# Rotary q and k turned by block squares and transfers instead of on TensorE, in a one-core decoder layer

## Chip, cores and metric

One NeuronCore of a Trainium2 chip runs the whole program. The metric is the device time of one execution in microseconds (us), as the median over runs. The core has five engines that run side by side, each with its own instruction queue: TensorE (PE, with its weight loads shown apart as PEld), VectorE (DVE), ScalarE (ACT), GpSimd (POOL) and SyncE (SP, which here only starts transfers).

## The reference

One layer of a decoder, on 256 tokens of width 1024, all in float32. A rotary mixer (branch a) and a stick-breaking mixer (branch b), both with 8 heads of 64, stand between two gated feed-forward halves:

```python
h = h + FFN_RES * swiglu(rms_norm(h, ffn1_norm), ffn1_w_gate, ffn1_w_up, ffn1_w_down)
u = rms_norm(h, mix_norm)
q_a, k_a, v_a, q_b, k_b, v_b, g_a, g_b = split(u @ w_in)
y_a = merge_heads(moba_attention(rotary(q_a), rotary(k_a), v_a))     # causal softmax
y_b = merge_heads(stick_breaking_attention(q_b, k_b, v_b))
gates = sigmoid(concatenate([g_a, g_b]) + b_gate)
h = h + (gate_a * (y_a @ w_branch_moba) + gate_b * (y_b @ w_branch_sb)) @ w_out
h = h + FFN_RES * swiglu(rms_norm(h, ffn2_norm), ffn2_w_gate, ffn2_w_up, ffn2_w_down)
out = rms_norm(h, final_norm)
```

The rotary turns the first 16 of each head's 64 columns by an angle that depends on the position.

## The kernel before

All weights are one stream of 376 tiles of 128x512. SP loads them in chunks of two tiles (512 KB) into `raw` buffers (`Weights.load`, L139 to L150; three buffers from chunk 12 on). `Weights.split` (L152) cuts each tile into a high part `wh` on ACT (L160 or L163) and the rest `wl` on DVE (L161 or L164), ten buffers of each. `unit` (L296) is the smallest step: three matmuls of 128x512, `wh` and `wl` by the activations' high part and `wh` by their low part (L292 to L294). After each unit `weave.tick()` counts one step and `W.pump()` splits one more tile, up to `AHEAD` = 7 tiles ahead of the tile in use. For 256 tokens each tile serves two units, t = 0 and t = 1.

The order of work on PE and SP is the order of the program, throughout. On ACT, DVE and POOL a planner sets the order in the middle of the kernel (from the end of the first feed-forward half to the start of the second) and the program in the rest. Side work is a set of Python generators in `Weave` (L92): each yields the number of steps after which it goes on, so `D_READY = 7` is a wait of seven units. Tasks added with `long=True`, the two attention lanes, advance at most one step between them per tick, and `flush(long=True)` runs whatever is left of them without units between.

Steps are counted here from the first unit of the mixer's input projection: blocks `in0` to `in9` of 16 units each (q_a, k_a, v_a, q_b, k_b, v_b and four blocks of gates, L874 to L890), so they are steps 1 to 160. Then come `ba` (y_a by its branch weights, steps 161 to 176, L901 to L917), `bb` (y_b, from step 177, L935 to L943) and `wo` (L948). In `in0` the t = 1 units come eight behind those of t = 0, elsewhere two; each block's two PSUM results (`acc_bank`, three buffers) are taken away by `evac`.

To be used in attention, q and k must stand with the head's columns on partitions. The kernel has two ways to turn them:

- For branch a (`rotary` true), `evac` copies the block to SBUF on ACT, `rotate` (L660) applies the rotary by four GpSimd operations (L666 to L669), and `turn` (L692) lets PE transpose eight 128x128 blocks by an identity into PSUM (L701), `D_TURN` = 10 steps after the second evacuation. ACT and DVE split the result into two parts (`split`, L312), and `D_READY` = 7 steps later it may be used.
- For branch b, DVE transposes 32x32 squares within 128x512 (L689) and `exchange` (L413) moves the squares between partitions by 16 transfers, alternately on SP's and GpSimd's queue, two a step. `D_LANDED` = 6 steps later the pieces are split.

The first column halves of the normalised activations after each feed-forward half and after the mixer go through `exchange` too (`Normed.moved`, L357: `uq`, `zq`); it puts 16 transfers of 16 KB a row block on the two queues.

The lanes (`lane`, L850) take head pairs 0 and 2, and 1 and 3: `moba_pair` (L765) for each as soon as q_a and k_a are there, then `stick_pair` (L809) as soon as q_b and k_b are. One `stick_pair` is scores `z`, three ACT operations, `sp`, cumulative sums (L834 to L836), the exponential `w` (L838), its split and `values` (L753), which makes `y_b`. The gates' sigmoids (L915) need another ACT table than the exponentials and are kept behind the last of them (`issue_after(marks["exp"])`).

`big` (L209) gives 24 SBUF buffers of 4 KB a partition to all the tiles of 128x1024.

Of the kernel before, what the change touches and what calls it, by code (L numbers as in the profile page):

```python
# [8 lines left out]
F32 = mybir.dt.float32  # L9
# [8 lines left out]
P = 128  # L18
# [10 lines left out]
CH = 2  # L29
# [8 lines left out]
D_TURNED = 3  # L38
D_MOVE = 2
D_MOVED = 12  # L40
D_LANDED = 6
D_PIECE = 2
D_TURN = 10
D_READY = 7
D_NORM = 4
D_SQUARES = 3
D_EIGHT = 6
# [81 lines left out]
class Weights:  # L129
# [9 lines left out]
    def load(self, n, tiles=0):  # L139

        n = min(n, N_TILES // CH)
        while self.loaded < n * CH + tiles:
            c, j = divmod(self.loaded, CH)
            if j == 0:
                nm = f"raw{c}"
                self.raw[c] = self.early(nm) if c < 12 else self.pool.tile([P, CH * 512], F32, name=nm, tag="raw", bufs=3)
            step = 1 if c < 4 else CH
            s = slice(j * 512, (j + step) * 512)
            self.nc.sync.dma_start(self.raw[c][:, s], self.stream[c, :, s])
            self.loaded += step  # L150

    def split(self):  # L152
        i = self.ready
        self.load(i // CH + 1)
        raw = self.raw[i // CH][:, i % CH * 512:i % CH * 512 + 512]
        hi = self.pool.tile([P, 512], F32R, name=f"wh{i}", tag="wh", bufs=self.bufs)
        lo = self.pool.tile([P, 512], F32R, name=f"wl{i}", tag="wl", bufs=self.bufs)
        g = self.gain(i)
        if g is None:
            self.nc.scalar.copy(hi, raw)  # L160
            self.nc.vector.tensor_sub(lo, raw, hi.bitcast(F32))  # L161
        else:
            self.nc.scalar.activation(hi, raw, AF.Copy, scale=g)  # L163
            self.nc.vector.scalar_tensor_tensor(lo, raw, g, hi.bitcast(F32), op0=ALU.mult, op1=ALU.subtract)  # L164
        self.parts[i] = hi, lo
        self.ready += 1
        if i % CH == CH - 1:
            del self.raw[i // CH]
            self.load(i // CH + 1 + 3)

    def pump(self):
        if self.ready < min(self.freed + self.bufs, self.at + self.ahead, N_TILES):
# [16 lines left out]
def hybrid_layer_kernel(ctx, tc, x, xt, pos, g_final, bgate, wstream, out):  # L189
# [17 lines left out]
        return psum.tile([P, 1024], F32, name=nm, tag="pr", bufs=2)  # L207

    def big(nm, dt=F32R):  # L209
        return work.tile([P, 1024], dt, name=nm, tag="big", bufs=24)  # L210

    def wide(nm, w=768):
        return work.tile([P, w], F32, name=nm, tag="f", bufs=4)
# [127 lines left out]
    class Normed:  # L341
# [15 lines left out]
        def moved(self, c):  # L357

            s = slice(c * 512, c * 512 + 512)
            q = big(f"{self.nm}q{self.t}{c}", F32)  # L360
            nc.vector.transpose(slots(q[:, 0:512], 4), plain(h[self.t][:, s]))
            yield D_SQUARES
            yield from exchange(q[:, 512:1024], q[:, 0:512], 4, [nc.sync, nc.gpsimd], 1)
            yield D_EIGHT
            split(plain(self.parts[0][:, s]), plain(self.parts[1][:, s]), slots(q[:, 512:1024], 4))
            self.there.add(c)
# [8 lines left out]
    class Given(Normed):  # L375
# [15 lines left out]
        def blk(self, k):  # L391
            o = k % 4 * T + self.t * P
            return [q[:, o:o + P] for q in self.made[k // 4 * 2:k // 4 * 2 + 2]]

    def lagged(n, lag):

# [9 lines left out]
    def slots(q, n):  # L406

        return q[:, 0:n * P].rearrange("p (g s w) -> p s g w", g=4, s=n)
# [15 lines left out]
    def ffn(base, xn, nm, on_half, lag, last=False):  # L424
# [5 lines left out]
        def hidden(b, t, bank):  # L430
# [10 lines left out]
            nc.vector.transpose(dst, plain(sh[:, 256:512]))  # L441
            if t == 1 and (b % 2 or b == FB - 1):
                weave.add(turn_hidden(p, n), D_TURNED)

        def later(f, *args):
            f(*args)
            return
            yield

        def turn_hidden(p, n):  # L450
            moved = big(f"hm_{nm}{p}", F32)
# [219 lines left out]
    def heads(b0, nm, res, rotary, diagonal):  # L671


        for j, which in enumerate("qk"):
            src = {}
            squares = None if rotary else big(f"{which}s{nm}", F32)

            def evac(t, ps, j=j, which=which, src=src, squares=squares):
                dst = row512(f"{which}{nm}{t}")
                if j == 0:  # L680
                    if nm == "a":
                        nc.gpsimd.tensor_scalar(rq[t], un[t].r, 0.125, None, op0=ALU.mult)
                    nc.scalar.activation(dst, ps, AF.Copy, scale=rq[t])
                else:
                    nc.scalar.activation(dst, ps, AF.Copy, scale=un[t].r)
                if rotary:
                    rotate(dst, t)
                else:
                    nc.vector.transpose(slots(squares, 8)[:, t:t + 7:2], plain(dst))  # L689
                src[t] = dst  # L690

            def turn(which=which, src=src, squares=squares):  # L692
                if rotary:
                    tp = two_banks(f"{which}tp{nm}")
                else:
                    tp = big(f"{which}m{nm}", F32)
                    yield from exchange(tp, squares, 8, [nc.sync, nc.gpsimd], 1)
                    yield D_LANDED
                for pr in range(4 if rotary else 0):
                    for t in range(2):  # L700
                        nc.tensor.transpose(tp[:, pr * 256 + t * P:pr * 256 + (t + 1) * P], src[t][:, pr * P:(pr + 1) * P], ident)  # L701
                if which != diagonal:
                    parts = big(f"{which}Th{nm}"), big(f"{which}Tl{nm}")
                    for c in range(2):
                        s = slice(c * 512, c * 512 + 512)
                        if rotary:
                            split(parts[0][:, s], parts[1][:, s], tp[:, s])
                        else:
                            split(plain(parts[0][:, s]), plain(parts[1][:, s]), slots(tp, 8)[:, c * 4:c * 4 + 4])
                            yield D_PIECE  # L710
                    ready = [[q[:, pr * 256:(pr + 1) * 256] for q in parts] for pr in range(4)]
                else:
                    tp4 = slots(tp, 8).rearrange("p (c t) g w -> p c t g w", t=2)
                    for c in range(2):
                        for j in range(2):
                            rows = slice(j * HD, j * HD + HD)
                            dst = [q[rows].rearrange("p (c j t g w) -> p c j t g w", c=2, j=2, t=2, g=4)[:, :, j] for q in res["bd"][c]]
                            split(dst[0], dst[1], tp4[rows, c * 2:c * 2 + 2])
                            yield D_PIECE
                    ready = [[q[:, pr % 2 * 512:pr % 2 * 512 + 512] for q in res["bd"][pr // 2]] for pr in range(4)]  # L720
                yield D_READY if rotary else D_READY - D_PIECE
                res[which] = ready

            if which == diagonal:
                res["bd"] = [(big(f"bdh{nm}{c}"), big(f"bdl{nm}{c}")) for c in range(2)]
                for c in range(2):
                    for q in res["bd"][c]:
                        for half in range(2):
                            q5 = q[half * HD:(half + 1) * HD].rearrange("p (c j t) -> p c j t", c=2, j=2)
                            nc.gpsimd.memset(q5[:, :, 1 - half, :].bitcast(F32), 0.0)  # L730
            project(b0 + j, evac)
            weave.add(turn(), D_TURN if rotary else D_TURNED)

        vs = big(f"vh{nm}"), big(f"vl{nm}")

        def evac_v(t, ps):
            s = slice(t * 512, t * 512 + 512)
            nc.scalar.activation(vs[0][:, s], ps, AF.Copy, scale=un[t].r)
            nc.vector.scalar_tensor_tensor(vs[1][:, s], ps, un[t].r, vs[0][:, s].bitcast(F32),
                                           op0=ALU.mult, op1=ALU.subtract)  # L740
            if t == 1:
                res["v"] = [[q[:, s * 512:(s + 1) * 512] for q in vs] for s in range(2)]

        project(b0 + 2, evac_v)
# [64 lines left out]
    def stick_pair(pr, b, y):  # L809
# [26 lines left out]
            nc.tensor.matmul(z0[:, :, 128:256], ones, s1, start=False, stop=i == 1, skip_group_check=True)  # L836
        w = wide(f"w{pr}")
        marks["exp"] = nc.scalar.activation(w, zz, AF.Exp).ins  # L838
        earlier(w)
        yield D_STICK[2]  # L840
        wh, wl = wide_r(f"wwh{pr}"), wide_r(f"wwl{pr}")
# [59 lines left out]
    for c in range(2):  # L901
        banks = {}
        for t, k in lagged(4, 2):
            if k == 0:
                banks[t] = acc_bank(f"ba{t}{c}")
            i = W_BR + c * 4 + k
            unit(banks[t], yk(ys["a"], k, t), W.get(i), k == 0, k == 3)
            if t == 1:
                W.done(i)
        if c == 0:  # L910
            weave.flush(long=True)
            with tc.issue_after(marks["exp"]):
                for br in range(2):
                    for t in range(2):
                        nc.scalar.activation(gates[br, t], gates[br, t], AF.Sigmoid)  # L915
        for t in range(2):
            nc.vector.tensor_mul(merged[t, c], banks[t], gate_half(0, t, c))  # L917

    mn = [None, None]

# [134 lines left out]
```

## Time and profile before

| | |
|---|---|
| median of 3 runs | 556.39 us (556.18 to 556.6) |
| the profiled execution's own time | 555.9 us |
| its span in the trace | 554.2 us |
| granted TensorE clock, mean over the span | 0.997 of full speed |
| busy share of the span: PE, PEld, DVE, ACT, POOL | 99%, 81%, 72%, 61%, 13% |
| DMA over the span | 111.69 MB, mean 202 GB/s |

The trace gives a start and a duration for each instruction. An engine that could not start has an idle time before it, and the trace names what ended it. Matmuls overlap in PE's pipeline, so a matmul's duration (390 ns for 512 columns) is more than its share of PE's time; the distance between the starts of two neighbours is that share. A row of a timeline with xN holds N instructions in a row. All numbers of an argument come from one profiled execution.

### The profile page before, as it was taken

The numbers are of one execution on the slowest core, as the hardware profiler recorded it, in microseconds if no ns is written. First come the engines' busy times: TensorE is split into PE (matmuls) and PEld (weight loads), VectorE is DVE, ScalarE is ACT, GpSimd is POOL, SyncE is SP. The second block draws the span as 40 slices with busy tenths as digits, with TensorE's granted clock in tenths as the row PEclk, the third lists the DMA queues.
The fourth block names the chain that finished last, engine by engine and source line by source line (L and its number), as shares of the span: only waits on it lengthen the run. The fifth ranks groups of instructions, "written<-read, shape, count | busy, mean of one in ns | idle before, by whom it ended". The sixth has DMA issues, their size and how long they took to land.

```text
span 554.2 us, 7853 instructions
## 1 busy us (share of the span) xinstructions
PE 546.1 (99%) x2494; PEld 449.5 (81%) x2494; DVE 401.3 (72%) x694; ACT 338.1 (61%) x576; POOL 70.1 (13%) x141
## 2 busy tenths in 40 slices
PE   9999999999999999999999999999999999999995
PEld 5788888888888888888888888888888888888884
DVE  6887788766466676889888888777677678655645
ACT  6865656655454767677875774476556566544633
POOL 1200000000003746022022200460000000000000
PEclk9999999999999999999999999999999999999998
DMA  8946766775685677455545464576657766757722
GB/s 311 403 141 202 220 216 216 220 237 184 210 235 179 200 232 220 155 159 183 176 151 172 137 202 149 179 242 216 219 180 234 238 206 200 229 179 230 243 79 76
DMA packets 42937, 111.69 MB, mean 202 GB/s; under 512 B 8080, under 2 KB 16528, under 8 KB 42896
## 3 DMA queue, kind: packets, MB, share of 16 engines
q1 hardware_dynamic: 40464, 107.90, 60.9%
q0 software_dynamic: 2000, 2.62, 1.8%
q10 hardware_dynamic: 432, 0.67, 0.3%
q8 instruction: 19, 0.31, 0.3%
q14 instruction: 22, 0.18, 0.1%
HBM read 102.25 MB, written 1.05 MB: 186 GB/s over the span
## 4 chain that ended last, share of the span: by engine, by line
PE 95%; DMA 3%; ACT 0%; DVE 0%; issue 0%; ACTq 0%
PE gu_f L293 14%; PE gu_f L294 14%; PE gu_f L292 14%; PE dn_f L294 7%; PE dn_f L292 7%; PE dn_f L293 7%; PE in L292 7%; PE in L294 7%; PE in L293 7%; DMA raw<-in_wstream 2%; PE wo L294 1%; PE wo L292 1%; PE wo L293 1%; PE y_a L748 1%; PE z L748 1%; PE y_b L748 1%
## 5 line engine op out<-in xcount | busy, mean ns | idle before, releaser
L164 DVE SCALAR_TENSOR_TENSOR wl<-raw,first,wh 128x512 fp32r<-128x512 f32 x256 | 181.8, 747 | 41.3 <-ACT wh L163 40.1
L163 ACT ACTIVATE wh<-raw,first 128x512 fp32r<-128x512 f32 x256 | 171.7, 717 | 56.3 <-DMA raw<-in_wstream 31.0
L160 ACT CAST wh<-raw 128x512 fp32r<-128x512 f32 x120 | 70.4, 620 | 63.9 <-DMA raw<-in_wstream 40.8
L161 DVE TENSOR_TENSOR wl<-raw,wh 128x512 fp32r<-128x512 f32 x120 | 78.6, 691 | 40.0 <-ACT wh L160 39.9
L292 PE MATMUL gu_f<-wh,zh 128*128 128x512 f32 x176 | 68.6, 390 | 0.0
L294 PE MATMUL gu_f<-wh,zl 128*128 128x512 f32 x176 | 68.5, 389 | 0.0
L293 PE MATMUL gu_f<-wl,zh 128*128 128x512 f32 x176 | 68.5, 389 | 0.0
L292 PE MATMUL dn_f<-wh,hth_f 128*128 128x512 f32 x172 | 67.1, 390 | 0.0
L294 PE MATMUL dn_f<-wh,htl_f 128*128 128x512 f32 x172 | 66.9, 389 | 0.0
L293 PE MATMUL dn_f<-wl,hth_f 128*128 128x512 f32 x172 | 66.9, 389 | 0.0
L292 PE MATMUL in<-wh,uh 128*128 128x512 f32 x160 | 63.5, 397 | 0.0
L293 PE MATMUL gu_f<-wl,xh 128*128 128x512 f32 x160 | 62.4, 390 | 0.3 <-DVE wl L164 0.3
L294 PE MATMUL in<-wh,ul 128*128 128x512 f32 x160 | 62.5, 391 | 0.0
L292 PE MATMUL gu_f<-wh,xh 128*128 128x512 f32 x160 | 62.4, 390 | 0.1
L293 PE MATMUL in<-wl,uh 128*128 128x512 f32 x160 | 62.4, 390 | 0.0
L294 PE MATMUL gu_f<-wh,xl 128*128 128x512 f32 x160 | 62.2, 389 | 0.0
L293 PEld LDWEIGHTS gu_f<-wl,zh 128*128 128x128 f32 x176 | 33.0, 188 | 6.9
L294 PEld LDWEIGHTS gu_f<-wh,zl 128*128 128x128 f32 x176 | 33.0, 188 | 6.8
L292 PEld LDWEIGHTS gu_f<-wh,zh 128*128 128x128 f32 x176 | 33.0, 188 | 6.8
L292 PEld LDWEIGHTS dn_f<-wh,hth_f 128*128 128x128 f32 x172 | 32.3, 188 | 6.9 <-DVE sh_f L433 0.4
L294 PEld LDWEIGHTS dn_f<-wh,htl_f 128*128 128x128 f32 x172 | 32.3, 188 | 6.7
L293 PEld LDWEIGHTS dn_f<-wl,hth_f 128*128 128x128 f32 x172 | 32.3, 188 | 6.7
(247 smaller groups left out, 756.5 us busy)
## 6 DMA issues: line engine op xcount, KB each, us to landing
raw<-in_wstream SPq DMA_DIRECT2D x184, 512.0 KB, 4.3
hm_f<-hs_f SPq DMA_DIRECT2D x160, 32.0 KB, 4.2
raw<-in_wstream SPq DMA_DIRECT2D x8, 256.0 KB, 4.9
h<-in_x SPq DMA_DIRECT2D x2, 512.0 KB, 6.6
bg<-in_bgate POOLq DMA_DIRECT2D x4, 256.0 KB, 4.6
xin<-in_xt SPq DMA_DIRECT2D x3, 256.0 KB, 5.1
hm_f<-hs_f SPq DMA_DIRECT2D x32, 16.0 KB, 3.1
gB<-in_g_final POOLq DMA_DIRECT2D x1, 512.0 KB, 6.2
```

The source lines that it names most:

```text
L160: self.nc.scalar.copy(hi, raw)
L161: self.nc.vector.tensor_sub(lo, raw, hi.bitcast(F32))
L163: self.nc.scalar.activation(hi, raw, AF.Copy, scale=g)
L164: self.nc.vector.scalar_tensor_tensor(lo, raw, g, hi.bitcast(F32), op0=ALU.mult, op1=ALU.subtract)
L292: nc.tensor.matmul(o, ah, wh, start=first, stop=False)
L293: nc.tensor.matmul(o, ah, wl, start=False, stop=False)
L294: nc.tensor.matmul(o, al, wh, start=False, stop=last)
L748: nc.tensor.matmul(o, a[p], b[q], start=first and i == 0, stop=last and i == 2, skip_group_check=True)
```

## The change

Both paths to attention are made alike. Rotary q and k are now transposed in 32x32 squares on DVE, `D_ROTATED` = 4 steps after their evacuation (a task `later(square, t, dst)`), and `exchange` moves the squares; the eight PE transposes of q and of k are gone. The exchange starts `D_ROTATED + D_SQUARED` = 7 steps after the second evacuation. Every exchange now deals its 16 transfers to GpSimd, SP, GpSimd in turn (11 and 5 instead of 8 and 8), three every two steps. `D_READY` is 5. A fourth `raw` buffer is loaded ahead from chunk 12 on; `big` has 23 buffers instead of 24, which is the same room. The long flush moves from the middle of `ba` to its end. Some lines of context are cut, nothing else.

```diff
-D_TURN = 10
-D_READY = 7
+D_ROTATED = 4
+D_SQUARED = 3
+D_READY = 5
...
-                self.raw[c] = self.early(nm) if c < 12 else self.pool.tile([P, CH * 512], F32, name=nm, tag="raw", bufs=3)
+                self.raw[c] = self.early(nm) if c < 12 else self.pool.tile([P, CH * 512], F32, name=nm, tag="raw", bufs=4)
...
         if i % CH == CH - 1:
             del self.raw[i // CH]
-            self.load(i // CH + 1 + 3)
+            self.load(i // CH + 1 + (4 if i // CH >= 12 else 3))
...
     def big(nm, dt=F32R):
-        return work.tile([P, 1024], dt, name=nm, tag="big", bufs=24)
+        return work.tile([P, 1024], dt, name=nm, tag="big", bufs=23)
...
-            yield from exchange(q[:, 512:1024], q[:, 0:512], 4, [nc.sync, nc.gpsimd], 1)
+            yield from exchange(q[:, 512:1024], q[:, 0:512], 4, [nc.gpsimd, nc.sync, nc.gpsimd], 2)
             yield D_EIGHT
...
+    def later(f, *args):
+        f(*args)
+        return
+        yield
...
         for j, which in enumerate("qk"):
-            src = {}
-            squares = None if rotary else big(f"{which}s{nm}", F32)
-
-            def evac(t, ps, j=j, which=which, src=src, squares=squares):
+            squares = big(f"{which}s{nm}", F32)
+
+            def square(t, src, squares=squares):
+                nc.vector.transpose(slots(squares, 8)[:, t:t + 7:2], plain(src))
+
+            def evac(t, ps, j=j, which=which, square=square):
...
                 if rotary:
                     rotate(dst, t)
+                    weave.add(later(square, t, dst), D_ROTATED)
                 else:
-                    nc.vector.transpose(slots(squares, 8)[:, t:t + 7:2], plain(dst))
-                src[t] = dst
-
-            def turn(which=which, src=src, squares=squares):
-                if rotary:
-                    tp = two_banks(f"{which}tp{nm}")
-                else:
-                    tp = big(f"{which}m{nm}", F32)
-                    yield from exchange(tp, squares, 8, [nc.sync, nc.gpsimd], 1)
-                    yield D_LANDED
-                for pr in range(4 if rotary else 0):
-                    for t in range(2):
-                        nc.tensor.transpose(tp[:, pr * 256 + t * P:pr * 256 + (t + 1) * P], src[t][:, pr * P:(pr + 1) * P], ident)
+                    square(t, dst)
+
+            def turn(which=which, squares=squares):
+                tp = big(f"{which}m{nm}", F32)
+                yield from exchange(tp, squares, 8, [nc.gpsimd, nc.sync, nc.gpsimd], 2)
+                yield D_LANDED
                 if which != diagonal:
                     parts = big(f"{which}Th{nm}"), big(f"{which}Tl{nm}")
                     for c in range(2):
                         s = slice(c * 512, c * 512 + 512)
-                        if rotary:
-                            split(parts[0][:, s], parts[1][:, s], tp[:, s])
-                        else:
-                            split(plain(parts[0][:, s]), plain(parts[1][:, s]), slots(tp, 8)[:, c * 4:c * 4 + 4])
-                            yield D_PIECE
+                        split(plain(parts[0][:, s]), plain(parts[1][:, s]), slots(tp, 8)[:, c * 4:c * 4 + 4])
+                        yield 1 if rotary else D_PIECE
...
-                yield D_READY if rotary else D_READY - D_PIECE
+                yield D_READY
                 res[which] = ready
...
-            weave.add(turn(), D_TURN if rotary else D_TURNED)
+            weave.add(turn(), D_ROTATED + D_SQUARED if rotary else D_TURNED)
...
         marks["exp"] = nc.scalar.activation(w, zz, AF.Exp).ins
+        b["w", pr] = True
         earlier(w)
...
         if c == 0:
-            weave.flush(long=True)
+            assert all(("w", pr) in b for pr in range(4))
             with tc.issue_after(marks["exp"]):
...
             nc.vector.tensor_mul(merged[t, c], banks[t], gate_half(0, t, c))
+    weave.flush(long=True)
```

## Rows read from the trace of the kernel before

**Rows 1.** The page's busy line: busy us, share of the span, instructions.

```profile
PE 546.1 (99%) x2494; PEld 449.5 (81%) x2494; DVE 401.3 (72%) x694; ACT 338.1 (61%) x576; POOL 70.1 (13%) x141
```

**Rows 2.** What PE waited for: engine, line, releaser, total us, times, longest.

```profile
PE warm L283 <- DVE zeros L262: 1.1, 1, 1.1
PE gu_f L293 <- DVE wl L164: 0.3, 1, 0.3
```

**Rows 3.** The chain that ended last, share of the span by engine (page).

```profile
PE 95%; DMA 3%; ACT 0%; DVE 0%; issue 0%; ACTq 0%
```

**Rows 4.** PE's timeline: start us, duration, engine, line, operation, [wait].

```profile
18.82 0.50 PE L293 MATMUL gu_f<-wl,xh 128*128 128x512 f32 x1 [0.29 <-DVE wl L164]
...
189.24 0.60 PE L353 MATMUL tp_u<-ident,h 128*128 128x128 f32 x4
...
193.10 0.39 PE L292 MATMUL in<-wh,uh 128*128 128x512 f32 x1
...
203.30 0.39 PE L292 MATMUL in<-wh,uh 128*128 128x512 f32 x1
...
204.67 1.04 PE L701 MATMUL qtpa<-ident,qa 128*128 128x128 f32 x8
...
210.35 0.39 PE L292 MATMUL in<-wh,uh 128*128 128x512 f32 x1
...
547.30 0.28 PE L294 MATMUL dn_f2p<-wh,htl_f 128*128 128x256 f32 x1
```

**Rows 5.** Groups of q's and k's transposes on PE: busy us, mean ns.

```profile
L701 PE MATMUL qtpa<-ident,qa 128*128 128x128 f32 x8 | 1.0, 272 | 0.0
L701 PE MATMUL ktpa<-ident,ka 128*128 128x128 f32 x8 | 1.0, 272 | 0.0
```

**Rows 6.** DVE's transposes of branch b's squares, min/median/max ns (line view).

```profile
L689 DVE STREAM_TRANSPOSE qsb<-qb x2: 705/705/705, 232.4 to 236.9; 128x512 f32<-128x512 f32 x2
```

**Rows 7.** Busy us by engine, 195 to 225 us: PE, PEld, DVE, ACT, POOL.

```profile
195.00:225.00 30.00, 30.00 (x149) 24.79 (x148) 21.62 (x31) 19.61 (x31) 14.18 (x26) 1.00 0.70 220
```

**Rows 8.** POOL's timeline: k's rotary operations, then branch b's loads, memsets and transfers.

```profile
208.95 0.47 POOL L666 TENSOR_TENSOR t_ka<-ka,cos 128x128 f32<-128x128 f32 x1 [7.38 <-ACT ka L685]
...
212.82 0.46 POOL L669 TENSOR_TENSOR ka<-t_ka,t_ka 128x128 f32<-128x128 f32 x1
213.23 1.16 POOL L882 DMA_DIRECT2D bg<-in_bgate  x2
...
217.82 1.08 POOL L730 MEMSET bdlb<- 64x512 f32 x2
237.93 4.15 POOL L418 DMA_DIRECT2D qmb<-qsb  x8 [19.03 <-DVE qsb L689]
```

**Rows 9.** Durations of the issues of `uq` on POOL, min/median/max ns (tile view).

```profile
L418 POOL DMA_DIRECT2D uq<-uq x16: 496/497/722, 173.7 to 182.7; - x16
```

**Rows 10.** DMA issues: KB each, median us from issue to landing.

```profile
uq<-uq SPq DMA_DIRECT2D x16, 16.0 KB, 3.1
uq<-uq POOLq DMA_DIRECT2D x16, 16.0 KB, 2.9
qmb<-qsb SPq DMA_DIRECT2D x8, 32.0 KB, 3.6
qmb<-qsb POOLq DMA_DIRECT2D x8, 32.0 KB, 4.0
```

**Rows 11.** The 151st tile: its low part on DVE, its first matmul.

```profile
201.72 0.75 DVE L164 SCALAR_TENSOR_TENSOR wl<-raw,first,wh 128x512 fp32r<-128x512 f32 x1 [0.47 <-ACT wh L163]
...
211.03 0.39 PE L292 MATMUL in<-wh,uh 128*128 128x512 f32 x1
```

**Rows 12.** What ACT's weight splits waited for: total us, times, longest.

```profile
ACT wh L160 <- DMA raw<-in_wstream: 40.8, 27, 3.7
...
ACT wh L163 <- DMA raw<-in_wstream: 31.0, 24, 3.0
```

**Rows 13.** From `uq` to `in0`: timeline of ACT and DVE, then PE.

```profile
183.84 0.60 ACT L313 CAST uh<-uq 128x512 fp32r<-128x512 f32 x1
184.91 0.69 DVE L314 TENSOR_TENSOR ul<-uq,uh 128x512 fp32r<-128x512 f32 x1 [0.61 <-DMA uq<-uq]
186.51 0.39 PE L292 MATMUL in<-wh,uh 128*128 128x512 f32 x1
```

**Rows 14.** The last `y_b`: its matmuls, its last split, its first use.

```profile
324.34 0.39 PE L748 MATMUL y_b<-wwh,vhb 128*128 128x512 f32 x1
...
325.25 0.28 PE L748 MATMUL y_b<-wwh,vlb 128*128 128x256 f32 x1
...
327.69 0.43 DVE L314 TENSOR_TENSOR ybl<-y_b,ybh 64x256 fp32r<-64x256 f32 x1
...
334.24 0.39 PE L292 MATMUL bb<-wh,ybh 128*128 128x512 f32 x1
```

**Rows 15.** ACT's timeline from the last exponential through the first sigmoid.

```profile
315.32 0.81 ACT L838 ACTIVATE w<-z 128x768 f32<-128x768 f32 x1 [0.36 <-PE z L836]
316.15 1.28 ACT L915 ACT_TABLE_LOAD   x1
317.44 1.06 ACT L915 ACTIVATE gate<-gate 128x1024 f32<-128x1024 f32 x1
```

More of the change, by code (lines that the diff above doesn't have):

```diff
@@ L443, in hidden @@
                 weave.add(turn_hidden(p, n), D_TURNED)
[L445 to L448, printed above, removed]
         def turn_hidden(p, n):
```

## The prediction

> **What bounds the kernel now.** I read the busy shares, then PE's own waits, then the chain of work that ended last. PE is busy for 546.1 of 554.2 us [rows 1]. That alone says little, since matmuls overlap; what decides is that PE waits twice in the whole execution, 1.1 us for its warm-up data and 0.3 us on a weight tile at 18.8 us, and never after [rows 2, 4]. The chain says the same: 95% of the span is PE, 3% the first transfers, ACT and DVE nothing [rows 3]. So from 19 us to PE's last matmul at 547 us [rows 4] the time is the sum of what PE has to stream. A change can take time out only by taking work off PE, and can add time only by making PE wait where it doesn't now. All idle time of ACT, DVE, POOL and the transfers is cover, and each move below is weighed against the cover that it uses up.
>
> **What leaves PE.** In a clean stretch 45 matmuls of 512 columns lie between starts at 193.10 and 203.30 us, so one costs 10.20 / 45 = 0.2267 us. From 203.30 to 210.35 us lie 27 matmuls and q's eight transposes: 7.05 us, less 27 x 0.2267 = 6.12, leaves 0.93 us for the transposes and for the slower starts just behind them [rows 4]. k's eight are the same group by count and duration [rows 5]. Sixteen transposes: 1.86 us off the path. Not less than 1.6, if some of the slower starts behind them belonged to something else; not more than 2.0, the two groups' busy time [rows 5]. I take 1.86. The 272 ns of one transpose is its time in the pipeline, not its price: eight of them at that would be 2.2 us, where 1.04 is the whole group's length [rows 4, 5].
>
> **What DVE and ACT get.** Four square transposes of 128x512, not in this trace for branch a, but the same instruction for branch b takes 0.705 us [rows 6]: 2.8 us on DVE between steps 12 and 36. In the 30 us around them DVE is busy 21.62 and ACT 19.61 [rows 7], so they fit. The splits of q and k stay four on each engine; they now read SBUF as the split of `uq` does, 0.60 and 0.69 us [rows 13], against PSUM before: about nothing either way, 0.1 us at most each. Cost on the path 0, because the weights are split ahead: the 151st tile's low part is done at 202.47 us and first read at 211.03 [rows 11], so an engine may come 8.6 us late there before PE notices.
>
> **What POOL gets.** The 22 new issues for q and k of branch a: one costs 4.15 / 8 = 0.52 us [rows 8], so 5.7 us for each exchange and 11.4 us together, where POOL has 30 - 14.18 = 15.8 us free [rows 7]. The order matters more. Step 23, where q's exchange begins, is at about 202.7 us (`in0` starts at 186.51 [rows 13]; 23 steps of three matmuls are 15.6; the four transposes of `tp_u` [rows 4] take half of 0.93). Eleven issues end at 208.4; k's rotary operations start at 208.95 before, 0.93 earlier after [rows 8]. They meet, but hardly. The last transfer lands 4.0 us later by the slower row [rows 10], at 212.4, and the split is due at step 39, 213.5 us. If the planner put q's last three issues behind k's rotary operations (208.95 to 213.28 [rows 8]), they would land at about 218, and ACT would stand for 4.5 us with weight splits and, six steps on, v's evacuation behind it. That is inside the 8.6 us for weights; for v's PSUM bank PE comes back six steps (4.1 us) after the evacuation is due, by which time ACT, two thirds busy, has made up part. 0 to 1 us; I take 0, since POOL issued eight in a row without a gap when their data was there [rows 8]. For k: rotary done at 212.4, two squares on DVE (which may stand for a microsecond behind step 36, at 211.5, with weight tiles behind it), 11 issues until 218.8, landed at 222.8; its split is due at step 55, 224.4 us. If the gates' bias loads and the memsets, which follow k's rotary on POOL today (213.23 to 218.90 [rows 8]), stay ahead of it, it lands 5.7 us later, 4.1 us past that step and inside the 8.6 us. 0 again. The lanes' own POOL work, the selections on `sp` and `w`, comes after step 108, when the last exchange (steps 83 to 93) has left the queue.
>
> **What SP gets.** Ten issues more for q and k, three fewer for each of branch b's two, six fewer for each of `uq` and `zq`: eight fewer in all. SP keeps program order, so a transfer that waits for its squares holds the weight loads behind it. The squares have three steps (2.0 us) between their instruction and the first transfer; a delay of DVE by a microsecond or two would move loads by less than that. The fourth `raw` buffer puts one more chunk in flight, two tiles or four steps, 2.7 us. It will shorten ACT's 40.8 and 31.0 us of waiting for `raw` [rows 12]. PE did not wait for that [rows 2], so its gain is 0, and it pays for the loads that get stuck.
>
> **What comes later.** Counted through the generators: q_a and k_a were usable at step 49 (32 + 10 + 7) and will be at 62 (32 + 7 + 10 + 6 + 2 + 5). The rotary pairs move 13 steps. The stick-breaking pairs don't: they wait for k_b, whose exchange takes 10 steps for 8, so the first `z` goes from step 106 to 108, the last cumulative sums from 154 to 162, the last `y_b` from 166 to 174. PE's work is the same, only elsewhere. Three covers get thin:
> The activations at `in0`: their exchange is two steps longer. Now the split of `uq` runs 183.84 to 185.60 us and PE comes at 186.51, for the low part at 186.97 [rows 13]. Two steps (1.36 us) later it would end at 186.96, just in time; one more weight tile of DVE (0.75 us [rows 11]) in front would cost 0.7 us. But the issues bound it less than that: 11 of 0.52 us from 173.7 us end at 179.4 and land at 182.3. 0, up to 0.7.
> The last `y_b`: from its last matmul's end (325.37) to its last split's end (328.12) is 2.75 us, and PE comes 6.1 us after that [rows 14]. After, five units lie between, 3.4 us to the high part and 3.85 to the low part: 1.1 us are left. A sigmoid of 1.06 us on ACT [rows 15] in between would use them up. 0, up to 1.
> The sigmoids: the last exponential starts 8 steps later with the previous `y_b` ahead of it: 315.32 + 5.44 + 1.03 [rows 14] - 1.86 = 319.9 us. The table and the first gate take 3.18 us [rows 15]: 323.1, and the product that frees a PSUM bank is done at 323.8. PE wants the bank at the twelfth unit of `ba`, about 325.9. 0.
> The long flush at step 176 finds nothing left. `big` with 23: I count at most 22 tiles alive at once (steps 83 to 160). 0.
>
> **Sum.** 554.2 - 1.86 = 552.3 us of span, 554.0 for the profiled execution's own 555.9. The median of the runs is 556.39, 0.5 above that execution; the same 1.86 off gives 554.5 us. Each cover that fails adds 0 to 1 us: 554.2 to 555.2 where at most one fails in part.
>
> **Rivals.** (a) A cover fails: the last `y_b`, v's bank and `uq` together may cost 0.8 to 2.7 us, and the gain is gone: 555.3 to 557.2. For it: `uq` and the last `y_b` are left with about a microsecond by the sums above, v's bank too if q lands late, and the order on ACT and DVE is a planner's. Against it: each needs a coincidence, and the slack elsewhere is 8 us.
> (b) Slower: GpSimd's issues stretch when DVE is busy. Place: k's chain, behind q's 11 issues on the same queue. With c us an issue, q's end at 202.7 + 11 c, k's rotary 4.3 later, k's squares 0.7, its own 11, landing 4.0: k is there at 211.7 + 22 c, against 224.4 for its split and 8.6 us more until the weights run out. PE stalls from c = 0.97, and the kernel is slower by over 0.2% from c = 1.1. At 1.25 (each issue behind one DVE weight tile, 0.50 + 0.75 [rows 9, 11]) k comes at 239.2, 6.2 us past the cover: 560.7 us. Against it: 16 issues of `uq` took 496 to 722 ns while DVE was splitting weights [rows 9], and landing is the same from both queues [rows 10]. At 0.72 each, k is 3.1 us late and PE sees nothing.
> The Trainium skill has the rule behind this, in "SBUF — State Buffer", section "SBUF: two separate sides": GpSimd writes the descriptors of its own transfers, and DVE operations that take both shared ports lock it out while they run. The same page measures 620 ns alone and 3100 ns beside DVE. Worked out from that page as an estimate, 22 issues of 3.1 us would bring k some 47 us past the cover, about 602 us. This trace doesn't agree for this mix of DVE work: none of these issues took over 722 ns [rows 9].
> (c) The change doesn't do all it says: the fourth buffer stays empty because SP stands behind a transfer. Then ACT's waits for `raw` stay, and PE, which doesn't see them, gives (the forecast) again.
>
> **Chances.** The forecast, (c) included, 0.72; gain under 554.0 us by something not seen here 0.02; (a) 0.19; (b) 0.07. About 0.2% (1.1 us) is what measurement can tell from no change. Faster: the forecast's range lies under 555.28, so 0.74. Same 0.19, slower 0.07. The range runs from 554.0 (2.0 off for the transposes, and 0.2 of spread of the runs on either median) to 556.2, which takes in the forecast's own 554.2 to 555.2 and the half of (a) in which one cover fails fully.
>
> **What would show it.** PE's waits after 19 us: none, as before. No L701; PE's instruction count down by 16 to 2478. First `S` 13 steps later, last `y_b` 8. ACT's waits for `raw` well under 72 us. GpSimd's issues still about 0.5 us. Wrong would be a wait of PE on `uh`, on `ybl`, on a PSUM bank at `ba`, or ACT standing for microseconds on the transfers of q or k with PE starved after.

## The result and the profile after

| | before | after |
|---|---|---|
| median | 556.38 us | 564.24 us (563.37 to 564.82) |
| ratio, 95% interval | | 1.0139 (1.0127 to 1.0152) |
| profiled execution, its span | 555.9, 554.2 us | 564.5, 562.8 us |

The change makes the kernel 7.9 us slower, where the forecast was 1.9 us faster. (The two profiled spans differ by 8.6 us; 0.7 of that is there by 30 us, in the first feed-forward half, where the trace of experiment ten, which changes nothing before q's transposes, is 0.5 us later too.) Of the page after: the busy line, and the chain by engine.

```profile
PE 548.1 (97%) x2478; PEld 448.7 (80%) x2478; DVE 403.6 (72%) x698; ACT 340.0 (60%) x576; POOL 88.2 (16%) x181
...
PE 84%; DMA 8%; DVE 2%; POOL 2%; issue 1%; ACT 1%; DVEq 0%; ACTq 0%; POOLq 0%
```

PE issues 16 fewer instructions than in [rows 1], as it should, but the chain is PE for 84% now instead of 95% [rows 3]: transfers, DVE, POOL and ACT have come into it. What PE waited for (engine, line, releaser, total us, times, longest):

```profile
PE ptp L788 <- DVE p L784: 3.4, 2, 2.8
PE in L293 <- ACT kb L688: 1.5, 1, 1.5
PE S L770 <- ACT kTha L314: 1.2, 1, 1.2
```

None of these stands in [rows 2]. They lie between 230 and 261 us. PE's timeline there, and before it the start of `in0`:

```profile
187.49 0.39 PE L294 MATMUL in<-wl,uh 128*128 128x512 f32 x1
188.00 0.50 PE L295 MATMUL in<-wh,ul 128*128 128x512 f32 x1
...
230.08 0.39 PE L295 MATMUL in<-wh,ul 128*128 128x512 f32 x1
231.68 0.39 PE L770 MATMUL S<-kTha,qTha 64*128 64x256 f32 x2 [1.21 <-ACT kTha L314]
...
242.19 0.85 PE L788 MATMUL ptp<-ident,p 128*128 128x128 f32 x6 [0.57 <-DVE p L784]
...
251.98 0.40 PE L295 MATMUL in<-wh,ul 128*128 128x512 f32 x1
253.88 0.50 PE L293 MATMUL in<-wh,uh 128*128 128x512 f32 x1 [1.50 <-ACT kb L688]
...
257.19 0.39 PE L295 MATMUL in<-wh,ul 128*128 128x512 f32 x1
260.36 0.85 PE L788 MATMUL ptp<-ident,p 128*128 128x128 f32 x6 [2.79 <-DVE p L784]
...
262.31 0.63 PE L294 MATMUL in<-wl,uh 128*128 128x512 f32 x1
262.74 0.63 PE L295 MATMUL in<-wh,ul 128*128 128x512 f32 x1
```

A small gap at `in0`, where PE comes to the low part of `uq` (0.51 us between starts, 0.3 over the pitch of 0.23), and four stops: the first `S` (starts 1.60 us apart from 230.08 on), the first pair's `ptp`, a unit that wants the PSUM bank of k_b's first block, and the second pair's `ptp` (3.17 us apart). Behind the last, starts come 0.43 us apart instead of 0.23. The granted clock says why (us of the window, busy us of PE, PEld, DVE, ACT and POOL, clock, DMA share, GB/s):

```profile
215.00:232.00 17.00, 15.79 (x71) 12.66 (x69) 9.99 (x16) 8.31 (x14) 10.60 (x21) 1.00 0.85 248
...
262.00:265.00 3.00, 3.00 (x9) 2.35 (x8) 2.50 (x7) 2.24 (x10) 2.26 (x5) 0.51 0.44 96
```

Behind this stop of 2.8 us the clock is granted at 0.51, the lower level of 1.2 GHz, for some three microseconds: eight pitches longer by 0.2, another 1.6 us. The gaps less their pitch (1.4 and 0.5 at `S`, 0.7, 1.7 and 2.9) and this 1.6 make 8.8 us. With the 0.3 at `in0`, and less the 1.9 of the transposes, that is 7.2 of the 7.9 us; the rest is not put down to single gaps.

Who was late? ACT's timeline through the same stretch:

```profile
215.92 1.15 ACT L314 CAST qTha<-qma 128x512 fp32r<-128x512 f32 x2 [3.90 <-DMA qma<-qsa]
...
231.01 1.14 ACT L314 CAST kTha<-kma 128x512 fp32r<-128x512 f32 x2 [4.92 <-DMA raw<-in_wstream]
...
250.85 1.78 ACT L314 CAST bdhb<-qmb 64x512 fp32r<-64x512 f32 x3 [6.17 <-DMA qmb<-qsb]
...
253.16 0.67 ACT L688 ACTIVATE kb<-in,r_u 128x512 f32<-128x512 f32 x1
...
254.87 0.46 ACT L780 ACTIVATE p<-S,st 128x256 f32<-128x256 f32 x1
```

ACT stands three times for an exchange: 3.9 us for q_a, 4.9 for k_a (the releaser named is a weight chunk, which this split doesn't read), 6.2 for q_b. The third is the costly one. Behind it, in ACT's order, stand k_b's evacuation (253.16), which frees PE's bank, and the second pair's exponentials (254.87). `ptp` waits for the normalisation of p, which DVE makes behind these exponentials and behind two low parts of q_b, from 258.84 to 260.41 us.

GpSimd's timeline for the exchanges of q_a and k_a:

```profile
204.68 3.98 POOL L424 DMA_DIRECT2D qma<-qsa  x8 [1.30 <-PE in L295]
209.17 0.50 POOL L424 DMA_DIRECT2D qma<-qsa  x1 [0.51 <-DMA qma<-qsa]
210.53 0.98 POOL L424 DMA_DIRECT2D qma<-qsa  x2 [0.87 <-DMA qma<-qsa]
...
214.87 1.13 POOL L877 DMA_DIRECT2D bg<-in_bgate  x2
216.66 2.95 POOL L424 DMA_DIRECT2D kma<-ksa  x6 [0.66 <-issue]
219.97 0.50 POOL L424 DMA_DIRECT2D kma<-ksa  x1 [0.35 <-DMA bg<-in_bgate]
222.99 1.11 POOL L424 DMA_DIRECT2D kma<-ksa  x2 [2.53 <-DMA bg<-in_bgate]
224.58 0.98 POOL L424 DMA_DIRECT2D kma<-ksa  x2 [0.48 <-DMA kma<-ksa]
```

Eight issues run through at 0.50 us each; the ninth waits for a landing. In the compiled program the transfers of this queue signal on eight semaphores in turn, and each waits until the one eight before it has landed. So an exchange of 11 waits for its own first pieces where they haven't landed by then, and k's seventh and eighth wait for the two bias loads, 256 KB each, that went ahead of them: the loads land at 219.69 and 222.71 us, and these issues follow 0.28 us later, at 219.97 and 222.99. Time from issue to landing (KB, median us):

```profile
qma<-qsa POOLq DMA_DIRECT2D x11, 32.0 KB, 5.0
kma<-ksa POOLq DMA_DIRECT2D x11, 32.0 KB, 6.5
...
qma<-qsa SPq DMA_DIRECT2D x5, 32.0 KB, 6.2
kma<-ksa SPq DMA_DIRECT2D x5, 32.0 KB, 7.2
```

The sum had 4.0 us, from branch b's exchanges [rows 10].

### The profile page after: what moved, and what is told of

The parts are those of the page before. It is cut to its first block, busy times and chain, and to the rows that moved or that the text cites. A ratio compares the mean times of both kernels' runs of the same rounds, so it can differ in the third digit from the quotient of the medians.

```text
span 562.8 us, 7879 instructions
## 1 busy us (share of the span) xinstructions
PE 548.1 (97%) x2478; PEld 448.7 (80%) x2478; DVE 403.6 (72%) x698; ACT 340.0 (60%) x576; POOL 88.2 (16%) x181
## 4 chain that ended last, share of the span: by engine, by line
PE 84%; DMA 8%; DVE 2%; POOL 2%; issue 1%; ACT 1%; DVEq 0%; ACTq 0%; POOLq 0%
PE gu_f L294 14%; PE gu_f L295 13%; PE gu_f L293 13%; PE dn_f L293 6%; PE dn_f L294 6%; PE dn_f L295 6%; PE in L295 4%; PE in L293 4%; PE in L294 4%; DMA raw<-in_wstream 3%; DMA kma<-ksa 2%; DMA uq<-uq 1%; PE wo L293 1%; PE wo L295 1%; PE wo L294 1%
## 5 line engine op out<-in xcount | busy, mean ns | idle before, releaser
L161 ACT CAST wh<-raw 128x512 fp32r<-128x512 f32 x120 | 71.7, 621 | 57.7 <-DVE wl L162 23.2
```

## The experiments

The theory after the traces: two separate losses. (1) k_a's exchange is late on GpSimd's queue, and PE waits at `S`. (2) On ACT the planner has put q_b's splits, which wait for their transfers, ahead of k_b's evacuation and the exponentials. Rivals: the fourth `raw` buffer, the deal of 11 and 5 as such, and that (2) is only (1) handed on. The kernel before took 556.4 to 556.5 us beside each of these runs.

**One: hold q_b's splits.** On the changed kernel, ACT's splits of q_b behind k_b's second evacuation:

```diff
+    marks[f"{which}{nm}"] = nc.scalar.activation(dst, ps, AF.Copy, scale=un[t].r).ins
...
-    split(dst[0], dst[1], tp4[rows, c * 2:c * 2 + 2])
+    with tc.issue_after(marks["kb"]):
+        split(dst[0], dst[1], tp4[rows, c * 2:c * 2 + 2])
```

> The changed kernel, with q_b's four splits on ScalarE held behind k_b's second evacuation; nothing else moves. In the changed kernel's trace ScalarE stands 6.2 us at the first of these splits (244.7 to 250.9 us) for q_b's transfers, with k_b's first evacuation and the second head pair's exponentials behind it, and PE then stalls three times for 7 us in all. Theory 1 (the order on ScalarE, made by the planner, puts a wait for transfers in front of work that PE needs): those stalls go, PE's wait of 2 us at the first S stays, 556.5 to 558.5 us. Theory 2 (weights starve because all engines are late, whatever stands first): under 2 us gained, 562 to 564.

Measured: 558.33 us, ratio 1.0043 (1.0026 to 1.0059): 5.9 us regained. PE's waits:

```profile
PE ptp L789 <- DVE p L785: 2.1, 2, 1.6
...
PE S L771 <- DVE kTla L315: 0.3, 1, 0.3
...
PE S L771 <- ACT kTha L314: 0.2, 1, 0.2
```

The wait for k_b's bank is gone, the second pair's `ptp` waits 1.6 us instead of 2.8, and the clock doesn't fall (mean 0.997 over the span; 0.993 in the changed kernel). The wait at `S`, expected to stay, is 1.0 us shorter too (0.5 us in two parts instead of 1.5). The edit doesn't touch k_a; in this execution its last piece lands at 229.3 us instead of 230.6. So about 1 of the 5.9 us may not be the edit's. One order on ACT was still worth most of the loss.

**Two: the bias loads leave GpSimd's queue.** On the changed kernel:

```diff
-    with tc.issue_after(marks["rot"]):
-        nc.gpsimd.dma_start(bg, ...)
+    nc.sync.dma_start(bg, ...)
```

> The changed kernel, with the four bias loads of 256 KB on SP's queue at their place in the program instead of GpSimd's, right ahead of k's exchange. ScalarE's order is the same. In the changed kernel k's 7th and 8th issues on GpSimd wait for the bias loads to land (2.5 us the longer), and the last issue comes at 225.1 us instead of some 222. Theory A (GpSimd's queue lets eight transfers be in flight, and k's exchange of eleven runs into that): last issue at about 222.5, the first S waits no more, 2 to 4 us gained (560 to 562), and more if the later stalls come from this delay. Theory B (the transfers land late because the transfer engines are full with a fourth chunk): little gained, 563 to 564.5, landing still near 6 us.

Measured: 561.20 us, ratio 1.0086 (1.0071 to 1.0101): 3.0 us regained. PE's waits:

```profile
PE ptp L788 <- DVE p L784: 3.2, 2, 2.8
PE in L293 <- ACT kb L688: 2.2, 1, 2.2
...
PE y_a L742 <- DVE yal L315: 0.9, 1, 0.9
```

No wait at `S` is left: k_a's last issue on GpSimd goes at 221.8 us instead of 225.1, and its last piece lands at 227.2 instead of 230.6. So the bias loads in the eight semaphores were what made k_a too late for PE. q_b's share is untouched. Its exchange begins at 237.46 us here, 3.5 us earlier than in the changed kernel, and ACT stands even longer for it:

```profile
248.68 1.13 ACT L314 CAST bdhb<-qmb 64x512 fp32r<-64x512 f32 x2 [7.54 <-DMA qmb<-qsb]
```

So (2) isn't (1) handed on. The clock stays at 1.00 in this trace, though PE stops for 2.8 us at the second pair's `ptp` as in the changed kernel; the 1.6 us of the half clock are among the 3.0, and the wait for `y_a` is new.

**Three: three `raw` buffers.** On the changed kernel:

```diff
-    tag="raw", bufs=4)
+    tag="raw", bufs=3)
...
-    self.load(i // CH + 1 + (4 if i // CH >= 12 else 3))
+    self.load(i // CH + 1 + 3)
```

> The changed kernel with three raw buffers and three chunks ahead as before; big stays at 23; ScalarE's order is the same. Theory B (the fourth chunk in flight makes the squares land late: 6.8 us for k where branch b's took 2.6 to 4.0 before): landing back to 4 us, the first S waits no more, 558 to 561 us. Theory A (the limit on GpSimd's queue) or the order on ScalarE: 563 to 565, no better, perhaps worse since weights are less far ahead when ScalarE stands.

Measured: 564.74 us, ratio 1.0147 (1.0132 to 1.0163): nothing regained. The wait at `S` goes, but only because PE has stopped before it, on the evacuation of v_a that stands on ACT behind a weight chunk. PE's wait:

```profile
PE in L293 <- DVE vla L733: 3.9, 1, 3.9
```

ACT's timeline at that chunk:

```profile
224.90 0.72 ACT L164 ACTIVATE wh<-raw,first 128x512 fp32r<-128x512 f32 x1 [5.14 <-DMA raw<-in_wstream]
```

k_a's pieces still land after medians of 5.8 and 6.3 us, so the fourth chunk isn't what makes them slow. Taking the fourth buffer away gives nothing back; in this trace ACT then comes to a stop at a load that comes late.

**Four: the old deal.** On the changed kernel, both exchange calls dealt turn about again, eight and eight:

```diff
-    yield from exchange(..., [nc.gpsimd, nc.sync, nc.gpsimd], 2)
+    yield from exchange(..., [nc.sync, nc.gpsimd], 1)
```

> The changed kernel with the transfers dealt SP, GpSimd in turn and two a step as before, for every exchange. Eight issues on GpSimd fit under a limit of eight. Theory A: q's exchange ends without a wait, k's waits only for the bias loads, k lands some 2 us sooner and is split two steps sooner by the program; 556 to 560 us. Theory B or the order on ScalarE alone: within 2 us of the changed kernel, 562 to 565.

Measured: 561.93 us, ratio 1.0098 (1.0081 to 1.0114): 2.3 us regained. The gap for `uq` at `in0` goes, and at `S` 0.5 us of waiting is left. The 556 to 560 us of Theory A are missed. ACT still stood for q_b, and with another order behind it PE waits once, for longer, and the clock is at half from 259.5 to 266.3 us. (The releaser named below is a weight split, which `ptp` doesn't read; what it needs is DVE's normalisation of p, whose third piece runs from 260.69 to 260.97 us.) ACT:

```profile
245.83 0.62 ACT L314 CAST bdhb<-qmb 64x512 fp32r<-64x512 f32 x1 [5.06 <-DMA qmb<-qsb]
```

PE's wait:

```profile
PE ptp L788 <- ACT wh L164: 4.2, 1, 4.2
```

**Five: both edits.** The first and the second together:

> Both edits of the two experiments above it: ACT's splits of q_b wait for k_b's second evacuation, and the gates' bias loads go to SP's queue. Theory of two separate losses: k's late exchange costs PE its wait at S (2.3 us, and 3.0 us with what follows), q_b's early splits cost it k_b's bank and p (5.9 us). Then the gains add: 564.2 - 5.9 - 3.0 = 555.3 us, 554.8 to 556.0, no gap of PE at S and none over 1 us at the second ptp. Rival: one loss seen twice (S late pushes p late, p late pushes the rest, and each edit only breaks the same chain at another link). Then one edit on top of the other gives little: 557.5 to 558.3 us, with a gap of 1 to 2 us at ptp still there.

Measured: 555.37 us, ratio 0.9982 (0.9973 to 0.9991). The gains add: 5.9 + 3.0 off 564.24 is 555.3. That they add to a tenth is in part luck: the half clock's 1.6 us are gone with either edit alone, about 1 us at `S` is gone with the first as well, and the second alone has some 2 us of other waits (k_b's bank, the third pair's `ptp`, `y_a`). What shows two losses is that neither edit alone clears PE's waits, and both do. PE's waits from the warm-up on:

```profile
PE warm L284 <- DVE zeros L263: 1.0, 1, 1.0
...
PE ptp L789 <- DVE p L785: 0.2, 1, 0.2
```

GpSimd's timeline of k_a's exchange:

```profile
216.10 3.96 POOL L424 DMA_DIRECT2D kma<-ksa  x8 [1.71 <-PE in L295]
220.56 1.47 POOL L424 DMA_DIRECT2D kma<-ksa  x3 [0.51 <-DMA kma<-ksa]
```

ACT's split of it:

```profile
226.76 1.14 ACT L314 CAST kTha<-kma 128x512 fp32r<-128x512 f32 x2 [4.25 <-DMA kma<-ksa]
```

The ninth issue still waits, for 0.51 us. ACT still stands 4.25 us for k_a, and it costs nothing now: k_a is there 4.2 us earlier than in the changed kernel, before PE asks for it.

**Six: both edits and the old deal,** that is the diffs of one, two and four.

> The kernel with both edits, and every exchange dealt as in the kernel before, turn about on SP and GpSimd (8 and 8 instead of 5 and 11). Theory: a third, separate loss is the wait at in0 for uq (0.5 us, 0.3 more than the pitch) and q's and k's last issues on GpSimd, since with 8 transfers of one exchange there no issue waits for a landing of its own exchange. Then 0.5 to 1.2 us less than with both edits: 554.2 to 554.8 us, which is the predicted gain of the transposes and no more. Rival: the deal is neutral once k has room, or the 30 issues that go back to SP's queue hold the weight loads: same time as with both edits, 555.0 to 556.0 us, with ACT's waits for raw up.

Measured: 556.14 us, ratio 0.9997 (0.9988 to 1.0005). The median is 0.8 us above that of both edits, but the intervals overlap and the profiled executions are alike (555.43 and 555.37). In the trace nothing waits at `in0`, and the third pair's `ptp` gap is 1.15 us, where it was 0.64. The rival holds so far: eight and eight for q and k shows no gain.

**Seven: the deal alone.** The kernel before with the diff of four the other way round, in both exchange calls:

> The kernel before, with nothing of the change but the deal: eleven of an exchange's sixteen transfers on GpSimd's queue, five on SP's, for uq, zq, q_b and k_b; rotary q and k stay on PE. Theory: a ninth transfer on GpSimd's queue waits for the landing of the first, so uq lands about a microsecond later and in0 waits 0.3 to 0.8 us; q_b and k_b land 1 to 2 us later, which the kernel before hides (its splits of q_b never waited). 556.7 to 557.3 us. Rival: the deal is what makes ACT stand behind q_b, too; then PE waits for k_b's bank and p as in the changed kernel, 559 to 562 us. If the deal costs nothing: 556.4 us.

Measured: 557.09 us, ratio 1.0010 (1.0000 to 1.0019). PE at `in0`:

```profile
187.88 0.39 PE L293 MATMUL in<-wl,uh 128*128 128x512 f32 x1
188.38 0.50 PE L294 MATMUL in<-wh,ul 128*128 128x512 f32 x1
```

0.51 us between starts instead of 0.23, the same gap as in the changed kernel, and no other wait of PE in the projections. So the deal costs 0.3 us through `uq` by the trace (the medians differ by 0.6), and doesn't by itself bring ACT to a stop that counts.

**Eight: both edits, `uq` and `zq` dealt eight and eight,** with four's diff in `Normed.moved` alone.

> The kernel with both edits (q_b's splits behind k_b, bias loads on SP), and uq and zq alone dealt eight and eight again. Theory: the 0.5 us gap at in0 comes from the ninth and later transfers of uq on GpSimd's queue; with eight it goes, the planner's order further on stays as it is with both edits. 0.3 to 0.5 us less than 555.4: 554.9 to 555.1 us, and no start-to-start gap over 0.4 us at in0. Rival: with both edits the rest of the loss is at ptp and in the run's own spread, and uq's gap only moved: 555.4 us again.

Measured: 555.13 us, ratio 0.9983 (0.9974 to 0.9991). The gap at `in0` is gone, but at the third pair's `ptp` the starts are now 1.09 us apart (0.64 with both edits): that takes the 0.3 us won at `in0` back, since PE comes earlier to a normalisation that isn't earlier. The medians differ by 0.24 us, which is inside the spread of the runs.

**Nine: one more step before `ptp`.** As eight, and:

```diff
-D_MOBA = (7, 5, 7)
+D_MOBA = (7, 6, 7)
```

> The same with the transposes of p one step later behind their normalisation (six steps instead of five). Theory: what is left behind the second S is 0.4 us at ptp, where PE comes before DVE has normalised p, and one step (0.7 us) covers it: 554.5 to 554.8 us, no gap over 0.4 us at ptp. Rival: a step more lets the planner order ACT and DVE otherwise, and another wait comes in its place: 555 to 557 us.

Measured: 556.25 us, ratio 0.9997 (0.9988 to 1.0005). The rival: nothing waits at `ptp`, but `y_a` waits 0.8 us for `pl` instead.

**Ten: the transposes' price.** The kernel before, each of the sixteen transposes of q and k made twice:

```diff
     nc.tensor.transpose(tp[...], src[t][...], ident)
+    nc.tensor.transpose(tp[...], src[t][...], ident)
```

> The kernel before with each of rotary q's and k's sixteen transposes on PE issued twice (the second writes the same again). It measures their price by itself. By the prediction's sum (0.93 us for eight, first of them paying for the slower starts behind them) 16 more cost 1.3 to 1.9 us: 557.7 to 558.2 us. Rival: a transpose costs its 272 ns in the pipeline, then 16 more cost 4.3 us: 560.7 us. If they run beside the matmuls' weight loads: under 0.5 us, 556.4 to 556.9 us.

Measured: 558.40 us, ratio 1.0036 (1.0024 to 1.0048): 2.0 us more. In the trace PE's offset against the kernel before rises by 0.9 us at q's group and by 0.9 at k's. The price in the sum, 1.86 us for sixteen, is right; 272 ns each would have been 4.3.

**Eleven: hold q_b's splits longer.** As eight, but behind the third pair's exponentials, and written ten steps later:

```diff
-    with tc.issue_after(marks["kb"]):
+    with tc.issue_after(marks["p2"]):
...
-    yield D_LANDED
+    yield D_LANDED + (10 if which == diagonal else 0)
```

> As the kernel with both edits and uq dealt eight and eight, but q_b's splits are held on ACT behind the third pair's exponentials instead of k_b's second evacuation (and written ten steps later, so that those exist). Theory: the 0.8 us wait of PE that is left (the third pair's ptp on DVE's normalisation) is the same loss once more: two low parts of q_b stand between that pair's row maxima and its normalisation on DVE. Moved behind it, no wait is left, and the time is the transposes' gain alone: 554.4 to 554.6 us. Rival: q_b's splits are then late for k_b's partner or push v_b's evacuation and k_b's splits, and PE waits there: 555.1 us or more.

Measured: 555.08 us, ratio 0.9978 (0.9969 to 0.9987), the lowest median, though not clear of eight's. PE's waits:

```profile
PE y_a L743 <- DVE yal L315: 0.5, 1, 0.5
```

Besides the warm-up and 0.5 us in the first feed-forward half, PE waits for nothing else. `ptp` doesn't wait; `y_a` does for 0.5 us, so the theory (no wait left, 554.4 to 554.6) misses by about that. The difference to the kernel before, 1.44 us of the medians, is about the 1.86 of the transposes less this wait.

**Twelve: the fourth `raw` buffer alone** on the kernel before: three's diff the other way round, and 23 buffers of `big`.

> The kernel before with nothing of the change but the fourth raw buffer (and the buffers of big from 24 to 23). Theory: PE never waited for raw, so nothing: 556.2 to 556.6 us, with ACT's waits for raw down from 72 us to a third or less. Rival: loads that start earlier collide with the exchanges and lift the landing times, as they may in the changed kernel: q_b's and k_b's transfers land 1 us later or more, 556.8 us or more.

Measured: 556.39 us, ratio 0.9999 (0.9990 to 1.0007). ACT's waits for `raw` fall from 71.8 us [rows 12] to 16.5, and PE gains nothing, as forecast.

## Why the prediction was wrong

**What leaves PE: right.** 1.86 us for the transposes; ten measures 2.0. When PE comes to the first `S` of the changed kernel, it is 2.4 us ahead of the kernel before (the same matmul starts at 230.08 instead of 232.51), the first pair's scores and `ptp`, which now come later, among it.

**What bounds the kernel, and the cover: right in method, wrong in use.** PE's own work did shrink, and only new waits could cost. But cover was reckoned per item that was moved, against the weights' 8.6 us [rows 11], and the weights never ran out.

**"What POOL gets", first failed step.** k_a was to land at 222.8 us; ACT's split of it starts at 231.01. The chain of the sum against the trace: q's exchange starts 2.0 us later (204.68 for 202.7); it takes 6.8 us for 5.7, with the ninth issue waiting for a landing (1.1); k's rotary is 0.6 faster; from there to k's first issue it is 1.7 us for 0.7, with the bias loads between (1.0); the eleven issues take 8.9 us for 5.7, with 3.4 us of waits for landings (3.2); the last lands 5.4 us later for 4.0 (1.4). Together 8.1 us. The price of an issue, 0.50 us, was right. What the sum lacked is that only eight transfers of this queue are in flight, which [rows 8] couldn't show: there every exchange had exactly eight. The bias loads were foreseen ahead of k, with the memsets, as a delay of 5.7 us, "4.1 us past that step and inside the 8.6 us. 0 again". There the step fails a second time: what k_a must meet is not the next weight tile but the first `S`, which PE reached at 230.3 us, and whose operands ACT and DVE still have to split. That cover is under 6 us from the due step at 224.4. Two takes this part alone away: 3.0 us, the half clock among it.

**"What comes later", second failed step, and the larger one: q_b's splits.** The prediction moved the rotary pairs by 13 steps and held that "PE's work is the same, only elsewhere". It looked for what ACT's standing would hold behind q_a and k_a, and for branch b reckoned only that the exchange is two steps longer, with effect on `z`. But q_b's splits, too, stand in an order that is fixed before the transfers run. In the kernel before the same splits waited for nothing, though the first of them stood ahead of k_b's evacuation there as well:

```profile
246.53 0.62 ACT L313 CAST bdhb<-qmb 64x512 fp32r<-64x512 f32 x1
...
248.35 0.68 ACT L685 ACTIVATE kb<-in,r_u 128x512 f32<-128x512 f32 x1
```

The second pair's exponentials were long done then (from 236.39 us). In the changed kernel ACT comes to q_b's splits at 244.7 us, with the transfers under way until 250.8, and stands 6.2 us; k_b's bank and the second pair's exponentials, 13 steps later now, are behind it. The late start of q_b's exchange (241.01 us instead of 237.93 [rows 8]) and its eleven issues aren't what decides: two starts it at 237.46, four has eight issues, and ACT stands 7.5 and 5.1 us. One takes the order away: 5.9 us, the half clock among it, and perhaps 1 us that isn't the order's. Which of the changes made the planner's order isn't settled by a run. Three and four still have q_b's splits ahead without the fourth buffer and without the deal, and seven shows that the deal alone doesn't bring the stop.

**What SP gets, and `raw`: right** for the kernel before (twelve). In the changed kernel three shows a 3.9 us wait of PE without the buffer, though with the rest of the loss in place the time is the same.

**The covers that were named: right.** `uq` costs 0.3 us at `in0` (0 to 0.7 forecast); PE has no wait on `ybl`, at the sigmoids, at v_a's bank, or for a buffer of `big`.

**Rivals.** (a) looked in the right manner (a cover fails, by a planner's order) at three other places. (b) had the right place, k's chain behind q's issues, and the sign, but its mechanism didn't come: issues of `qma` and `kma` took 496 to 562 ns on GpSimd, and the stops are waits for landings. The rule of the Trainium skill that stood beside it ("SBUF — State Buffer", section "SBUF: two separate sides": GpSimd is locked out while DVE uses both shared ports) has no part in this loss by these rows.

**The sum, had it been right.** Five and eleven give the forecast's mechanism its due: 555.37 and 555.08 us, against the forecast's 554.5. The traces put the rest down to waits of 0.3 to 0.5 us, at `in0` and `ptp` in five and at `y_a` in eleven.

## What to carry to other kernels

Where an engine's order is written before transfers land, ask of each instruction that waits for one what stands behind it on that engine, and reckon the cover from the first consumer that PE reaches, not from the resource that has the most slack. Before moving transfers to a queue, count how many it has in flight at once and what large ones are among them. When a change loses, hold the one instruction that stands first: here two edits of order brought back 8.9 us, more than the 7.9 that had been lost.

## What the runs showed that was not expected

- From the ninth on, transfers on GpSimd's queue waited for the landing of the one eight before: 1.4 us in all for q_a's eleven in the changed kernel, 0.5 us for k_a's in five, and 3.4 us with two loads of 256 KB among the eight. q_b's eleven went out in 5.37 us without a stop; there the first piece had landed, after 1.7 us, before the ninth was issued.
- Landing of a 32 KB piece went from medians of 3.6 and 4.0 us [rows 10] to 5.0 to 7.2 us where the DMA share was 0.83 to 0.89 (203 to 232 us).
- Behind a stop of PE of 2.8 us the granted clock was 0.51 from 262 to 265 us, and pitches were 0.43 us. It fell with the stops of 3.9 and 4.2 us in three and four as well. In two it stayed at 1.00 behind a stop of the same 2.8 us.
